# An encoder layer on one core: squares of x moved behind the last rounding of the first gate's input, transposes moved ahead, one product copied by ScalarE

## The chip, the core and the metric

One NeuronCore of one Trainium2 chip. The metric is the device time of one execution of the whole kernel in microseconds, the median of several runs. The engines are named as in the profile: PE is TensorE (matmuls), PEld its weight loads, DVE VectorE, ACT ScalarE, POOL GpSimd, SP SyncE, which only issues DMAs here. Each engine works through its own instructions in order.

## The reference

x is 512 x 2048 in float32, one batch and one layer.

```
h  = rms_norm(x, pre_mix_g);  z = h @ w_in                      # [q | k | v | u]
m  = concat(chunked_attention(q, k, v), multiscale_pool(u)) @ w_o
x  = x + rms_norm(m, post_mix_g)
h  = rms_norm(x, pre_ffn_g)
up = causal_dwconv(h @ w_up)                                    # 2048 x 11264, 3 taps
y  = (gelu(up[:, :5632]) * up[:, 5632:]) @ w_down               # 5632 x 2048
x  = x + rms_norm(y, post_ffn_g)
```

## The kernel before, in words

**Products.** Every float32 operand is split into a rounded high part and the rest (`split`, lines 133 to 141: ScalarE rounds on line 135, or on 138 with a gain per channel; VectorE subtracts on line 136, or 139). A product of a pair is three matmuls, high x high, low x high and high x low (`mm3`, lines 151, 153, 154; the first needs only the high parts, and the second of the gate's matmuls needs the low part of the activations). The larger products are Winograd's form of Strassen's scheme: seven products P1 to P7 of half-size blocks, whose sums VectorE, ScalarE and accumulating DMAs make.

**The order of the work.** TensorE's order is the order of the code. The order on the other engines is planned when the program is built, from modelled times: an instruction of later code can go ahead of one of earlier code that isn't ready. `tc.issue_after(ins)` gives each instruction traced in its block an edge of order to `ins`, if it is on the engine of `ins`; no semaphore is waited on for that. Buffers are tiles in rings: a new tile waits until the readers of the one whose place it takes are done. PSUM has eight banks, each a tile of 128 x 512.

**The first gate (lines 705 to 786).** After the output projection's last product, the rows of x are finished in two halves of 256 tokens. For each half `norm` makes the scale, `x2` (line 715) adds the normed projection to x, `turn_back` (lines 723 to 733) transposes x block by block on TensorE and rounds it into the tiles `gT` with the gain (lines 138, 139), and `keep_x` (lines 717 to 721) squares x on ScalarE for the next norm, two halves of a row block at a time through one scratch tile `junk` (lines 643 to 645), and stores x by SP. The squares' sums are added on line 787; the factor from them is used only behind the second `up` product's start, when `spread2` transposes it (line 213, tile `R`).

The first unit's gate, h @ w_up, is made in two halves of tokens so that it can begin before the second half of x is there (`gate_part(q, t0)`, lines 762 to 767): four weight blocks q of four channel blocks each, two output blocks j, so 24 matmuls of 256 columns for a q and half. The code makes all four parts of the first half; then in five steps it adds x (`x2`, columns of step q), transposes four channel blocks of the second half (8 transposes), and from the second step on multiplies the part of the step before. The first 16 transposes so stand side by side on TensorE. `keep_x(2)` stands behind these steps in the code. Behind the gate come the first unit's other product (`ups[1]`, line 785) and the sums of `gT` for Winograd's scheme (line 1028).

**The first chunk of the down projection (lines 876 to 926 and 1296 to 1312).** The contraction over 5632 is cut into five chunks of 1024 and a rest. In a chunk there are seven products for each of two column halves cc, 24 matmuls of 512 columns each (`multiply`). In chunk 0 their order is `ORDER0`: P1 of both halves, P2 of both, P5, P6, P3, P7, P4. Products accumulate in chains of two banks: P1, P6, P7 and P4 in `pa`, P5 and P3 in `pg`, P2 in `pd`. With P1's two chains kept open, P2's four banks are the ones that P5 takes next: P5 of the second half waits until `pd` of the second half is read. `keep_product` reads the banks: P1, P5 and P6 are copied by ScalarE (`copied`, line 900); for P2 and P3 VectorE adds the banks to the copy kept before (line 909). The copies are tiles of a ring of five, `part`. The result is added to a DRAM sum by a DMA that GpSimd issues (lines 923, 925). Factors are made `AHEAD` = 3 products in advance, so that the roundings for the products to come (`bh`, `bl`, `ah`, `al`) stand in the code ahead of a product's `keep_product`.

**The end.** `last` makes the last rest's blocks of 128 rows; the final row block has columns cut 512, 512, 512, 256, 256. When its norm is known, line 1403 adds each piece to x on VectorE and line 1404 stores it by SP. The pieces are taken in order of their width, the narrowest first.

Of the kernel before, what the change touches and what calls it, by code (L numbers as in the profile page):

```python
# [17 lines left out]
D = 2048  # L18
# [21 lines left out]
V_PREFFN = V_PREMIX + KD  # L40
# [5 lines left out]
def f32(ap):  # L46
    return ap.bitcast(F32)
# [28 lines left out]
def encoder_layer(ctx: ExitStack, tc: tile.TileContext, x, xT, vecs, rel, post_mix, post_ffn,  # L76
# [7 lines left out]
    nc = tc.nc  # L84
# [16 lines left out]
    def bank(name):  # L101
        return psum.tile([P, 512], F32, tag="ps", name=name)
# [27 lines left out]
    def col(v, i):  # L130
        return vec[:, v + i:v + i + 1]

    def split(hi, lo, src, scale=None):
        if scale is None:
            rounded = nc.scalar.activation(hi, src, AF.Copy)  # L135
            rest = nc.vector.tensor_sub(lo, src, f32(hi))  # L136
        else:
            rounded = nc.scalar.activation(hi, src, AF.Copy, scale=scale)
            rest = nc.vector.scalar_tensor_tensor(lo, src, scale, f32(hi), op0=ALU.mult, op1=ALU.subtract)
        split.last, split.rest = rounded.ins, rest.ins  # L140
        return rounded.ins
# [35 lines left out]
    def new_hT(name):  # L177

        return [new_pair(f"{name}{i}", 4, S) for i in range(4)]
# [7 lines left out]
    def new_gT():  # L187
        return [big.tile([P, 4, 4, S // 2], F32R, tag="hT", bufs=4, name=f"gT{i}") for i in range(4)]

    def g_half(gT, kb, t):  # L190
        return tuple(gT[kb // 4][:, kb % 4, at, :] for at in AT[t])
# [5 lines left out]
    def part(w, *idx):  # L197
        return tuple(v[(slice(None),) + idx] for v in w)
# [24 lines left out]
    def qk_specs(h):  # L223
        return halves(f"q{h}", w_in, head_cols("q", h), 8, P), halves(f"k{h}", w_in, head_cols("k", h), 8, P)
# [45 lines left out]
    for h in range(1, HEADS):  # L270
        q, k = qk_specs(h)
# [57 lines left out]
    hT = new_hT("hT")  # L329
# [5 lines left out]
    for kb in range(KD):  # L335
        i, o = divmod(kb, 8)
# [22 lines left out]
    with tc.tile_pool(name="p1", bufs=2, reuse_waits="tile") as p1:  # L359
# [216 lines left out]
        T = S // 2  # L576
# [41 lines left out]
    with tc.tile_pool(name="p2", bufs=1, reuse_waits="tile") as p2:  # L618
# [9 lines left out]
        ssq2, rm = (small[:, i:i + 8].rearrange("p (a b) -> p a b", a=NT) for i in (16, 24))  # L628
# [3 lines left out]
        def columns(cc):  # L632
            return slice(cc * 512, (cc + 1) * 512)
# [9 lines left out]
        def square(v, total):  # L643
            junk = p2.tile([P, D // 2], F32, tag="junk", name="junk")
            nc.scalar.activation(junk[:, :v.shape[-1]], v, AF.Square, accum_out=total)
# [59 lines left out]
        xn = {}  # L705
# [8 lines left out]
                v = xn[t0 + t][:, l * D // 2 + cs.start:l * D // 2 + cs.stop]  # L714
                nc.vector.scalar_tensor_tensor(v, y[:, t, cs], rm[:, t0 + t, l:l + 1], v, op0=ALU.mult, op1=ALU.add)

        def keep_x(t0):
            for t in range(t0, t0 + 2):
                for l in range(2):
                    square(xn[t][:, l * D // 2:(l + 1) * D // 2], ssq2[:, t, l:l + 1])  # L720
                nc.sync.dma_start(x2d[t - 2] if t >= 2 else out[t * P:(t + 1) * P, :], xn[t])

        def turn_back(t0, pair):

            ps = bank(f"xt{t0}_{pair}")
            for k in range(2):
                kb = 2 * pair + k
                for t in range(2):
                    nc.tensor.transpose(ps[:, k * T + t * P:k * T + (t + 1) * P],
                                        xn[t0 + t][:, kb * P:(kb + 1) * P], ident)  # L730
            for k in range(2):
                kb = 2 * pair + k
                split(*g_half(hT, kb, t0 // 2), ps[:, k * T:(k + 1) * T], col(V_PREFFN, kb))

        whole = slice(0, D // 2)
        for cc in range(2):
# [4 lines left out]
        hT = new_gT()  # L741
# [17 lines left out]
        ups = [[bank(f"up0_{p}_{j}") for j in range(2)] for p in range(2)]  # L759
        gate_w = []  # L760

        def gate_part(q, t0):
            sl = slice(t0 * P, t0 * P + T)
            for kb in range(4 * q, 4 * q + 4):
                for j in range(2):
                    mm3(ups[0][j][:, sl], part(gate_w[q], j, slice(kb % 4 * P, (kb % 4 + 1) * P)), g_half(hT, kb, t0 // 2),
                        kb == 0, kb == KD - 1)

        for q in range(4):
            gate_w.append(weights.get(f"w00_{q}", 3 - q))  # L770
            gate_part(q, 0)
        for q in range(5):
            if q < 4:
                x2(2, (y21, y22)[q // 2], q // 2, columns(q % 2))
                for i in range(2):
                    turn_back(2, 2 * q + i)
            if q:
                gate_part(q - 1, 2)
                weights.prefetch(q)
        keep_x(2)  # L780
        for q in range(4):
            w = weights.get(f"w10_{q}")
            for kb in range(4 * q, 4 * q + 4):
# [109 lines left out]
    def keep_product(c, cc, i):  # L893

        ps = chains[cc, CHAIN[i]]

        def copied():
            v = later["part"]("part")
            for t in range(2):
                nc.scalar.activation(v[:, t, :], ps[t], AF.Copy)  # L900
            return v

        if i in (1, 5, 6):
            kept[cc, i] = copied()
            return
        if i in (2, 3):
            v = kept.pop((cc, {2: 1, 3: 6}[i]))
            for t in range(2):
                nc.vector.tensor_add(v[:, t, :], ps[t], v[:, t, :])  # L909
        else:  # L910
            v = copied()
            if i == 7:
                five = kept.pop((cc, 5))
                nc.vector.tensor_add(flat(v), flat(five), flat(v))
        if i in (2, 3, 4):
            del chains[cc, CHAIN[i]]
        n = ENDS[i]
        if (c, cc) == (NC - 1, 1) and i in (2, 4):
            not_stored[n] = v
            return  # L920
        dest = sums[n][:, cc * S:(cc + 1) * S].rearrange("(t p) n -> p t n", p=P)
        if (n, cc) in begun:
            nc.gpsimd.dma_start(dest, v, accum_op=ALU.add)  # L923
        else:
            nc.gpsimd.dma_start(dest, v)
            begun.add((n, cc))

    def flat(v):
        return v.rearrange("p a b -> p (a b)")

    with tc.tile_pool(name="p3", bufs=2, reuse_waits="tile") as p3:
# [74 lines left out]
        T = S // 2  # L1006
# [218 lines left out]
    with tc.tile_pool(name="p4", bufs=2, reuse_waits="tile") as p4:  # L1225
# [138 lines left out]
        parts, scaled, ssqs, befores = [[] for _ in range(NT)], [[] for _ in range(NT)], {}, {}  # L1364

        def last(t, cols):
            ps = bank(f"yl{t}")[:, :cols.stop - cols.start]
            for i in range(2):
                last_block(ps, i, t, cols)
            if not parts[t]:  # L1370
                ssqs[t] = piece("ssq", 3, 5)
            ssq, n = ssqs[t], len(parts[t])
            v = y[t][:, cols]
            width = cols.stop - cols.start
            (nc.vector.tensor_add if cols.stop <= C else nc.vector.tensor_sub)(v, ps, v)
            junk = product_part("junk").rearrange("p a b -> p (a b)")
            nc.scalar.activation(junk[:, :width], v, AF.Square, accum_out=ssq[:, n:n + 1])
            if cols.start % C == 0 and t < 2:
                scaled[t].append(row((slot_h, slot_l)[t], f"vg{t}"))
            elif cols.start == 0:  # L1380
                v2 = right_tile(("wl", "wh")[t - 2], f"vg{t}", F32).rearrange("p a b -> p (a b)")
                scaled[t] += [v2[:, :C], v2[:, C:]]
            vg = scaled[t][cols.start // C][:, cols.start % C:cols.start % C + width]
            last.mul = nc.vector.tensor_mul(vg, v, gains[cols.start // C][:, cols.start % C:cols.start % C + width]).ins
            parts[t].append((cols, vg))
            if cols.stop < D and blocks(t)[n + 1].stop == D:
                befores[t] = piece("s3", 3, 1)
                nc.vector.reduce_sum(befores[t], ssq[:, :n + 1], axis=AX.X)
                nc.vector.tensor_scalar(befores[t], befores[t], 1.0 / D, EPS, op0=ALU.mult, op1=ALU.add)
            if cols.stop < D:  # L1390
                return
            r = piece("s1", 3, 1)
            nc.vector.scalar_tensor_tensor(r, ssq[:, n:n + 1], 1.0 / D, befores[t], op0=ALU.mult, op1=ALU.add)
            nc.gpsimd.tensor_tensor(r, r, mhalf[:, :1], op=ALU.pow)
            if t < 2:
                for i in range(2):
                    v = scaled[t][i]
                    nc.scalar.activation(v, v, AF.Copy, scale=r)
                    nc.gpsimd.dma_start(out[t * P:(t + 1) * P, i * C:(i + 1) * C], v, accum_op=ALU.add)
                return  # L1400
            for cols, vg in sorted(parts[t], key=lambda p: p[0].stop - p[0].start):
                res = x2_last[t - 2][cols.start // 1024][:, cols.start % 1024:(cols.stop - 1) % 1024 + 1]
                nc.vector.scalar_tensor_tensor(res, vg, r, res, op0=ALU.mult, op1=ALU.add)
                nc.sync.dma_start(out[t * P:(t + 1) * P, cols], res)

        for n in ("11", "12", "21", "22"):
            for t in range(2):
                at = y[t + 2 * int(n[0]) - 2]
                l = int(n[1]) - 1
                load_sum(n, t, at[:, l * C:(l + 1) * C])  # L1410
                if n in not_stored:
                    v = at[:, l * C + S:(l + 1) * C]
# [56 lines left out]
```

## Time and profile before

| | us |
|---|---|
| three timed runs, median (lowest to highest) | 1881.79 (1881.34 to 1882.3) |
| the profiled execution | 1885.39 |
| its span, first to last instruction | 1883.6 |
| TensorE busy in the span | 1868.9 |
| VectorE busy | 1417.9 |
| ScalarE busy | 1001.6 |
| GpSimd busy | 287.0 |

The mean granted clock of TensorE is 0.997 of full speed. In lines of the profile, "out<-in" are tiles by their names in the program, x16 means that 16 instructions are merged in the row, and a bracket at the end is the idle time of the engine just before and what ended it. A timeline row has the start and the length in us; matmuls overlap, so the length of one is more than the step from one to the next.

### The profile page before, as it was taken

What the parts mean: (1) busy time and instruction counts of PE and PEld (TensorE: products, weight loads), DVE (VectorE), ACT (ScalarE), POOL (GpSimd) and SP (SyncE); (2) the same over time, 40 slices, a digit from 0 to 9 for tenths busy, and PEclk for the clock granted to TensorE, in tenths of its full rate; (3) what the DMA queues carried; (4) which work ended last, traced back from release to release, by engine and by line L of the source; (5) the groups of instructions that cost most, each with busy time, mean ns of one, the idle gap of its engine ahead of it and who ended that gap; (6) DMA issues with size and microseconds to landing.
All of it is one profiled execution on the core that took longest, in us unless ns stands there. A gap on an engine that the chain in (4) does not pass through costs nothing.

```text
span 1883.6 us, 24695 instructions
## 1 busy us (share of the span) xinstructions
PE 1868.9 (99%) x9438; PEld 1595.4 (85%) x9438; DVE 1417.9 (75%) x1608; ACT 1001.6 (53%) x1261; POOL 287.0 (15%) x388
## 2 busy tenths in 40 slices
PE   9999999999999999999999999999999999999998
PEld 7888888888888888888888888888888788888886
DVE  5554445587598657888888888888887799889886
ACT  6333333346465345656656666665665665565553
POOL 4301011000000102121121212222121011111111
PEclk9999999999999999999999999999999999999999
DMA  8799599359796948889888888988889877876885
GB/s 295 244 251 239 159 266 239 105 151 330 225 301 221 241 145 188 204 203 204 199 203 200 207 208 199 199 199 209 209 172 298 325 230 178 206 201 169 181 232 156
DMA packets 181990, 404.47 MB, mean 215 GB/s; under 512 B 11312, under 2 KB 62384, under 8 KB 176560
## 3 DMA queue, kind: packets, MB, share of 16 engines
q0 software_dynamic: 50384, 150.49, 41.5%
q1 hardware_dynamic: 131488, 252.41, 40.0%
q8 instruction: 74, 1.21, 0.3%
q14 instruction: 44, 0.36, 0.1%
HBM read 356.72 MB, written 96.47 MB: 241 GB/s over the span
## 4 chain that ended last, share of the span: by engine, by line
PE 96%; DVE 1%; ACT 1%; DMA 1%; issue 0%; SPq 0%; POOL 0%; POOLq 0%; DVEq 0%; ACTq 0%
PE qa L159 14%; PE qa L165 8%; PE qg L159 7%; PE pa L153 4%; PE pa L154 4%; PE pa L151 4%; PE qg L165 4%; PE qd L159 4%; PE m L154 3%; PE m L153 3%; PE m L151 3%; PE up L153 2%; PE up L154 2%; PE up L151 2%; PE pg L151 2%; PE pg L153 2%
## 5 line engine op out<-in xcount | busy, mean ns | idle before, releaser
L159 PE MATMUL qa<-gT,wfh 128*128 128x512 f32 x912 | 228.3, 392 | 0.0
L136 DVE TENSOR_TENSOR wfl<-wx,wfh 128x1024 fp32r<-128x1024 f32 x152 | 185.9, 1223 | 52.8 <-ACT wfh L135 37.2
L135 ACT ACTIVATE wfh<-wx 128x1024 fp32r<-128x1024 f32 x152 | 161.0, 1059 | 118.6 <-PE qg L159 46.4
L159 PEld LDWEIGHTS qa<-gT,wfh 128*128 128x128 f32 x912 | 164.1, 189 | 29.4
L1092 POOL DMA_DIRECT2D wx<-in_w_up x113 | 96.9, 857 | 451.3 <-DVE wfl L136 430.1
L159 PE MATMUL qg<-h,wfh 128*128 128x512 f32 x608 | 150.4, 389 | 0.1
L136 DVE TENSOR_TENSOR bl<-b,bh 128x2048 fp32r<-128x2048 f32 x56 | 126.9, 2287 | 17.3 <-ACT bh L135 11.7
L135 ACT ACTIVATE bh<-b 128x2048 fp32r<-128x2048 f32 x56 | 106.1, 1914 | 62.4 <-DVE b L859 26.4
L159 PEld LDWEIGHTS qg<-h,wfh 128*128 128x128 f32 x608 | 113.9, 188 | 23.9 <-ACT zb L1149 0.5
L135 ACT ACTIVATE wfh<-wy 128x1024 fp32r<-128x1024 f32 x76 | 80.6, 1061 | 93.1 <-PE qg L159 53.0
L165 PE MATMUL qa<-gT,wfl 128*128 128x256 f32 x912 | 127.7, 283 | 0.0
L151 PE MATMUL pa<-bh,ah 128*128 128x512 f32 x320 | 124.5, 389 | 0.0
L153 PE MATMUL pa<-bl,ah 128*128 128x512 f32 x320 | 124.5, 389 | 0.0
L154 PE MATMUL pa<-bh,al 128*128 128x512 f32 x320 | 124.5, 389 | 0.0
L165 PEld LDWEIGHTS qa<-gT,wfl 128*128 128x128 f32 x912 | 119.9, 191 | 3.3 <-ACT zm L1153 0.2
L136 DVE TENSOR_TENSOR wfl<-wy,wfh 128x1024 fp32r<-128x1024 f32 x76 | 92.8, 1221 | 5.6 <-PE qa L159 1.5
L136 DVE TENSOR_TENSOR wfl<-wz,wfh 128x1024 fp32r<-128x1024 f32 x38 | 46.6, 1227 | 55.3 <-PE qa L159 52.2
L165 PEld LDWEIGHTS qg<-h,wfl 128*128 128x128 f32 x608 | 82.9, 190 | 5.9
L165 PE MATMUL qg<-h,wfl 128*128 128x256 f32 x608 | 84.8, 282 | 0.0
L923 POOL DMA_DIRECT2D sum<-part x30 | 36.2, 1206 | 262.4 <-DVE part L909 194.7
L159 PE MATMUL qa<-h,wfh 128*128 128x512 f32 x304 | 76.1, 392 | 0.0
L159 PE MATMUL qd<-gT,wfh 128*128 128x512 f32 x304 | 75.1, 389 | 0.0
(541 smaller groups left out, 4702.4 us busy)
## 6 DMA issues: line engine op xcount, KB each, us to landing
wx<-in_w_up POOLq DMA_DIRECT2D x113, 512.0 KB, 6.0
b<-in_w_down SPq DMA_DIRECT2D x32, 1024.0 KB, 7.0
wx<-in_w_up SPq DMA_DIRECT2D x40, 512.0 KB, 5.5
wz<-in_w_up SPq DMA_DIRECT2D x38, 512.0 KB, 5.9
wy<-in_w_up SPq DMA_DIRECT2D x38, 512.0 KB, 4.6
wy<-in_w_up POOLq DMA_DIRECT2D x38, 512.0 KB, 5.8
sum<-part POOLq DMA_DIRECT2D x38, 512.0 KB, 8.0
wt<-in_w_o POOLq DMA_DIRECT2D x16, 1024.0 KB, 11.6
```

The source lines that it names most:

```text
L135: rounded = nc.scalar.activation(hi, src, AF.Copy)
L136: rest = nc.vector.tensor_sub(lo, src, f32(hi))
L151: nc.tensor.matmul(ps, l[0], r[0], start=first, stop=False, skip_group_check=onto)
L153: nc.tensor.matmul(low, l[0], r[1], start=False, stop=False, skip_group_check=onto)
L154: nc.tensor.matmul(ps, l[1], r[0], start=False, stop=last, skip_group_check=onto)
L159: nc.tensor.matmul(ps, w[0][:, kb], pairs[kb][0], start=fresh and not kb, stop=last, skip_group_check=not fresh)
L165: nc.tensor.matmul(ps[:, sl], w[1][:, kb], pair[:, sl], start=False, stop=last, skip_group_check=not fresh)
L923: nc.gpsimd.dma_start(dest, v, accum_op=ALU.add)
L1092: nc.gpsimd.dma_start(self.raw[k, what], self.block(k, m, kh), accum_op=ALU.add)
```

## The change

```
-        def keep_x(t0):
+        def keep_x(t0, behind=None):
             for t in range(t0, t0 + 2):
                 for l in range(2):
-                    square(xn[t][:, l * D // 2:(l + 1) * D // 2], ssq2[:, t, l:l + 1])
+                    with tc.issue_after(behind) if behind else nullcontext():
+                        square(xn[t][:, l * D // 2:(l + 1) * D // 2], ssq2[:, t, l:l + 1])
...
-                split(*g_half(hT, kb, t0 // 2), ps[:, k * T:(k + 1) * T], col(V_PREFFN, kb))
+                turn_back.last = split(*g_half(hT, kb, t0 // 2), ps[:, k * T:(k + 1) * T], col(V_PREFFN, kb))
...
-        def gate_part(q, t0):
+        def gate_part(q, t0, some=slice(0, 4)):
-            for kb in range(4 * q, 4 * q + 4):
+            for kb in range(4 * q + some.start, 4 * q + some.stop):
...
         for q in range(4):
             gate_w.append(weights.get(f"w00_{q}", 3 - q))
-            gate_part(q, 0)
+            if q < 3:
+                gate_part(q, 0)
+        gate_part(3, 0, slice(0, 2))
         for q in range(5):
             if q < 4:
                 x2(2, (y21, y22)[q // 2], q // 2, columns(q % 2))
                 for i in range(2):
                     turn_back(2, 2 * q + i)
+            if not q:
+                gate_part(3, 0, slice(2, 4))
             if q:
                 gate_part(q - 1, 2)
                 weights.prefetch(q)
-        keep_x(2)
+        keep_x(2, turn_back.last)
...
         if i in (2, 3):
             v = kept.pop((cc, {2: 1, 3: 6}[i]))
-            for t in range(2):
-                nc.vector.tensor_add(v[:, t, :], ps[t], v[:, t, :])
+            if (c, cc, i) == (0, 1, 2):
+                other = copied()
+                nc.vector.tensor_add(flat(v), flat(other), flat(v))
+            else:
+                for t in range(2):
+                    nc.vector.tensor_add(v[:, t, :], ps[t], v[:, t, :])
...
-            for cols, vg in sorted(parts[t], key=lambda p: p[0].stop - p[0].start):
+            for cols, vg in sorted(parts[t], key=lambda p: p[0].start - p[0].stop):
```

The four squares of the second half of x get an edge behind the last ScalarE rounding of `turn_back`. The last part of the first half's product is cut in two, 12 matmuls each, with the first 8 transposes of the second half between them; the next 8 follow the second 12. P2 of the second column half in chunk 0 is copied out of its banks by ScalarE into a tile of the ring `part` of its own, and VectorE adds that tile to the kept copy. The last row block's pieces are added and stored widest first.

## The prediction

> **What bounds the kernel now.** I read the page first, then TensorE's waits, then the busy time by stretches around each wait, and last the instructions in order of time there.
>
> ```profile
> span 1883.6 us, 24695 instructions
> PE 1868.9 (99%) x9438; PEld 1595.4 (85%) x9438; DVE 1417.9 (75%) x1608; ACT 1001.6 (53%) x1261; POOL 287.0 (15%) x388
> PE pg L151 <- DVE part L909: 2.0, 1, 2.0
> PE up L151 <- ACT gT L138: 1.7, 1, 1.7
> 576.00:580.00 4.00, 2.32 (x20) 1.96 (x18) 3.02 (x6) 2.49 (x6) 0.00 (x0) 1.00 0.38 156
> 580.00:584.00 4.00, 3.71 (x19) 3.23 (x18) 2.58 (x9) 4.00 (x11) 0.36 (x1) 0.74 0.94 395
> 1472.00:1476.00 4.00, 2.10 (x10) 1.41 (x8) 4.00 (x5) 3.83 (x4) 0.00 (x0) 1.00 1.04 397
> 1476.00:1480.00 4.00, 3.90 (x10) 3.15 (x11) 4.00 (x4) 2.00 (x2) 0.72 (x1) 0.57 1.06 429
> ```
>
> TensorE is busy 99% of the span, so only its own waits and its clock are worth anything. Two waits stand out, 1.7 us before the first gate product and 2.0 us in the first chunk of the down projection. In the stretches (length, then PE, PEld, DVE, ACT, POOL, granted clock, DMA share, GB/s) each is followed by a fall of the granted clock, to 0.74 and to 0.57 of four microseconds. Of all 4 us stretches of the span these are the only places, and what adjoins them, with a clock under 0.99 ahead of the last microseconds. The change touches both places, and the order of the last stores.
>
> **Part 1, the first gate.** In order of time:
>
> ```profile
> 573.22 0.28 PE L151 MATMUL up<-gT,w_3h 128*128 128x256 f32 x1
> 573.31 5.38 DVE L715 SCALAR_TENSOR_TENSOR x<-y,small,x 128x512 f32<-128x512 f32 x8
> 576.10 1.91 PE L729 MATMUL xt<-ident,x 128*128 128x128 f32 x16
> 578.13 1.06 ACT L645 ACTIVATE junk<-x 128x1024 f32<-128x1024 f32 x1 [1.51 <-DVE x L715]
> 579.18 0.46 ACT L138 ACTIVATE gT<-xt,vec 128x256 fp32r<-128x256 f32 x1
> 579.67 0.48 DVE L139 SCALAR_TENSOR_TENSOR gT<-xt,vec,gT 128x256 fp32r<-128x256 f32 x1 [0.98 <-ACT gT L138]
> 579.69 0.38 PE L151 MATMUL up<-gT,w_0h 128*128 128x256 f32 x1 [1.68 <-ACT gT L138]
> 580.21 0.39 PE L153 MATMUL up<-gT,w_0h 128*128 128x256 f32 x1
> 582.17 0.41 PE L153 MATMUL up<-gT,w_0h 128*128 128x256 f32 x1
> 582.38 0.41 PE L154 MATMUL up<-gT,w_0l 128*128 128x256 f32 x1
> 585.34 1.04 PE L729 MATMUL xt<-ident,x 128*128 128x128 f32 x8
> 586.14 0.37 PE L151 MATMUL up<-gT,w_1h 128*128 128x256 f32 x1
> 589.90 0.36 PE L151 MATMUL up<-gT,w_2h 128*128 128x256 f32 x1
> ```
>
> The transposes are done by about 577.9, but ScalarE stands in a square of x (578.13) that itself waited 1.51 us for VectorE's eight residual sums, and rounds the first transposed block only at 579.18. TensorE resumes at 579.69, waits again for the low part (580.21), and from about 582 runs at a step of 0.21 us where the product before it made 24 matmuls in 576.10 - 573.22 = 2.88 us, 0.12 each. The whole loss: 16 transposes and 24 matmuls took 585.34 - 576.10 = 9.24 us here; the same work one step later (8 transposes, 24 matmuls, 8 transposes, from 585.34 to 589.90) took 4.56. So **4.7 us** are lost, of which about 1.7 to the half clock.
>
> The change takes the four squares out of the way and sends the first 8 transposes ahead of the last 12 matmuls of the half product. TensorE reaches them at 573.22 + 12 x 0.12 = 574.66. They need the first two residual sums: eight in 5.38 us, one of 0.745, is a step of 0.66, so the second ends at about 574.72. I charge 0.2 us of waiting. Transposes to 575.7 (8 in 586.14 - 585.34 = 0.80), 12 matmuls to 577.1, 8 transposes to 577.9; one more change between the two kinds costs 0.1 (589.90 - 585.34 less 2 x 0.80 and 2.88 is 0.08). ScalarE, with nothing ahead, rounds block 0 by 576, so the high part is in time.
>
> The low part is VectorE's, and the residual sums hold VectorE to 578.69. If all eight stay ahead, the low part of block 0 ends at 578.69 + 0.48 = 579.17 and TensorE idles about 1.25 us; if it is put among them as soon as it is ready (about 576), nothing. The gain is 4.7 - 0.3 - 1.25 = 3.1 or 4.7 - 0.3 = 4.4. VectorE's order is the planner's, and no row of before shows which it is: at 576 four of the eight sums are still to come, so the low part can fall between them, perhaps a sum or two late. I take **3.7**, the middle.
>
> The moved squares: four of 1.06 us, each with a read of its sum, now start behind the last rounding near 593 and end by about 602 even if every weight rounding goes first. Who waits:
>
> ```profile
> 596.09 1.06 ACT L135 ACTIVATE w_3h<-w_3r 128x1024 fp32r<-128x1024 f32 x1 [2.09 <-PE up L153]
> 606.92 0.39 PE L151 MATMUL up<-gT,w_2h 128*128 128x512 f32 x1
> 623.40 0.44 PE R L213 x4
> ```
>
> Behind them in ScalarE's queue stands the rounding of 596.09 and one like it just before, whose blocks are first used at 606.92 or later, 10 us of cover and more; VectorE's sum of the squares and GpSimd's root are needed at 623.40, more than 20 us later. Both uses come some 4 us earlier after the change; the cost is still nothing. The two stores of x on SP's queue read x alone and don't wait for the squares. If the cover were gone, it would cost at most the 4.3 us of the squares.
>
> **Part 2, the second P2.** In the first chunk:
>
> ```profile
> 1468.50 0.39 PE L151 MATMUL pg<-bh,ah 128*128 128x512 f32 x1
> 1473.72 0.39 PE L154 MATMUL pg<-bh,al 128*128 128x512 f32 x1
> 1476.10 0.65 PE L151 MATMUL pg<-bh,ah 128*128 128x512 f32 x1 [2.00 <-DVE part L909]
> 1483.26 0.39 PE L151 MATMUL pa<-bh,ah 128*128 128x512 f32 x1
> 1474.13 1.22 DVE L136 TENSOR_TENSOR al<-s,ah 128x1024 fp32r<-128x1024 f32 x1
> 1475.27 1.28 DVE L909 TENSOR_TENSOR part<-pd,part 128x512 f32<-128x512 f32 x2
> 1472.05 1.06 ACT L135 ACTIVATE ah<-s 128x1024 fp32r<-128x1024 f32 x1 [0.98 <-DVE s L1263]
> 1473.02 1.90 ACT L135 ACTIVATE bh<-t 128x2048 fp32r<-128x2048 f32 x1
> 1474.82 1.06 ACT L900 ACTIVATE part<-pg 128x512 f32<-128x512 f32 x2
> ```
>
> The product that ended at 1468.50 leaves its two banks to the one due at 1473.95 (24 matmuls, a step of 5.22/23 = 0.227). VectorE empties them only at 1475.27, behind operations for later products, the last of them that of 1474.13. The product then runs from 1476.10 to 1483.26, 7.16 us instead of 5.45, since the clock is half for a part. Loss: 1483.26 - 1473.95 - 5.45 = **3.86 us**.
>
> With the change ScalarE copies (2 x 0.53 us as in the row of 1474.82) and VectorE adds from SBUF later, 1.22 us in place of 1.28. The copies are ready at 1468.5. In the order of the code they stand behind the rounding of 1472.05 and ahead of that of 1473.02; the last place that gives ends the first copy at 1473.6, before the bank is wanted. Ahead of that, all is hidden. ScalarE has 1.06 us more to do; what it delays, the rounding of 1473.02, is for a product that starts after 1484. I take **3.8**, with 0 if they fall behind 1473.02.
>
> **Part 3, the last stores**, not in the title but in the diff:
>
> ```profile
> 1877.23 2.87 DVE L1403 SCALAR_TENSOR_TENSOR x<-vg,s,x 128x256 f32<-128x256 f32 x5 [0.72 <-POOL s L1394]
> 1880.12 0.33 SPq L1404 DMA_DIRECT2D out<-x  x1
> out<-x SPq DMA_DIRECT2D x7, 256.0 KB, 2.4
> out<-x SPq DMA_DIRECT2D x2, 128.0 KB, 2.0
> ```
>
> The same five sums end at the same time; the last store has 128 KB, 2.0 us to landing instead of 2.4. Three large stores before it could still be under way, so I take 0.3 (0 to 0.4).
>
> **The sum** is 3.7 + 3.8 + 0.3 = 7.8 us. The profiled execution took 1885.39 us (span 1883.6), the three timed runs have a median of 1881.79; a wait of TensorE weighs the same in both, so 1885.39 becomes 1877.6 and the median 1881.79 - 7.8 = **1874.0**. The terms' ends are 3.1 to 4.4, 3.6 to 3.9 and 0 to 0.4, so 1873.1 to 1875.1.
>
> **Rivals.**
> (1) *VectorE takes ScalarE's place and the clock still falls*: all eight sums stay ahead, 1.25 us of idling, and 1.7 us of half clock remain. Total gain 1.4 + 3.8 + 0.3 = 5.5: 1876.3. Against it: 1.25 us is under the 1.7 and 2.0 us that went ahead of the two falls. [...]
> (2) *The half clock is not the idling's doing* and comes at both places anyway. 1.7 us at each stay: gain 7.8 - 3.4 = 4.4, 1877.4. [...] Against it: the only two long waits are the only two falls.
> (3) *Part 2 does nothing*, because the planner sets the copies behind the rounding of 1473.02: the bank is free at about 1475.4, as before. Gain 4.0: 1877.8.
> (4) *Slower*: the copy takes one of the five tiles of the ring "part".
>
> ```profile
> 1493.65 1.28 ACT L900 ACTIVATE part<-pa 128x512 f32<-128x512 f32 x2 [2.35 <-PE pa L154]
> 1494.83 1.91 ACT L135 ACTIVATE bh<-t 128x2048 fp32r<-128x2048 f32 x1
> DMA to landing us min/median/max: 3.1/7.8/8.4
> ```
>
> The copy of 1493.65 then needs the tile of this P2, which is free when VectorE has added and its store has landed, some 8 us more. Behind it on ScalarE stands the rounding of 1494.83, for the product due at about 1506.6. With 1.1 + 1.9 + 2.3 us of copy and roundings the store must land by 1501 and the sum be made by 1493, else TensorE waits by as much. Nothing holds VectorE's sum any more, so the planner may leave it late; past about 1501 all 7.8 us are lost, and at 1505 the time is 1886. Against it: VectorE made it at 1475 before.
> (5) *The change does not do what it says*: the new edges or the moved transposes leave the order as it was, 1881.5. The edge is between two operations of ScalarE, so this is hardly likely.
>
> **Chances.** Forecast 0.66, (1) 0.09, (2) 0.05, (3) 0.08, (4) 0.08, (5) 0.04. A measurement can tell about 0.2% from no change, 3.8 us: faster means under 1878.0. (3) lies on that bound, half to each side: faster 0.66 + 0.09 + 0.05 + 0.04 = 0.84, same 0.04 + 0.04 = 0.08, slower 0.08. The range goes from 1872.6, all terms at their best with half a microsecond for the spread of runs, to 1878.2, which takes in (1), (2) and most of (3), and leaves out (4) and (5).
>
> **What would show it.** In the changed profile: no wait "up <- gT" over 0.7 us and no "pg <- part" at all among TensorE's waits; granted clock 1.00 throughout until the tail; squares on ScalarE behind 590, eight transposes near 574.8; two copies out of pd on ScalarE before 1470; 128x256 sums last. The forecast is wrong if a new wait of TensorE over 1 us appears in either place, or if a fall of the clock stands where no wait is.

## The result, and the profile after

| | before | after |
|---|---|---|
| median of 11 timed runs, us | 1882.45 | 1877.71 |
| lowest to highest, us | 1881.34 to 1883.78 | 1876.59 to 1881.26 |
| span of the profiled execution, us | 1883.6 | 1876.5 |

The ratio is 0.9977, 95% interval 0.9967 to 0.9986: by the ratio faster by 4.3 us (2.6 to 6.2); the medians differ by 4.7. Forecast were 1874.0 us and a gain of 7.8; 1877.71 lies in the range, near its upper end. The spans of the two profiled executions differ by 7.1 us, much more than the medians. That gap is what the experiments are about.

From the page of the changed kernel and the list of TensorE's waits (line, what it waited for: us in total, times, longest):

```profile
span 1876.5 us, 24700 instructions
PE 1864.2 (99%) x9438; PEld 1592.8 (85%) x9438; DVE 1418.1 (76%) x1607; ACT 1002.3 (53%) x1263; POOL 287.1 (15%) x388
PE qa L165 <- ACT zm L1162: 0.9, 1, 0.9
PE up L153 <- DVE gT L139: 0.6, 1, 0.6
```

Both long waits of before are gone. At the gate a wait for VectorE's low part has come in place of that for ScalarE; in the first chunk there is none. (The wait of 0.9 us on L165 stands at 819 us, in a stage that the change leaves alone; in a second profile of this kernel it is not there.)

The gate in order of time, changed kernel:

```profile
572.94 5.38 DVE L715 SCALAR_TENSOR_TENSOR x<-y,small,x 128x512 f32<-128x512 f32 x8
573.33 0.28 PE L151 MATMUL up<-gT,w_3h 128*128 128x256 f32 x1
574.77 1.04 PE L730 MATMUL xt<-ident,x 128*128 128x128 f32 x8
575.41 0.92 ACT L138 ACTIVATE gT<-xt,vec 128x256 fp32r<-128x256 f32 x2 [4.97 <-PE xt L730]
577.07 1.04 PE L730 MATMUL xt<-ident,x 128*128 128x128 f32 x8
577.86 0.36 PE L151 MATMUL up<-gT,w_0h 128*128 128x256 f32 x1
578.25 0.87 DVE L139 SCALAR_TENSOR_TENSOR gT<-xt,vec,gT 128x256 fp32r<-128x256 f32 x2
578.78 0.38 PE L153 MATMUL up<-gT,w_0h 128*128 128x256 f32 x1 [0.55 <-DVE gT L139]
589.27 1.05 ACT L645 ACTIVATE junk<-x 128x1024 f32<-128x1024 f32 x1
592.30 0.40 PE L151 MATMUL up<-gT,w_0h 128*128 128x512 f32 x1
```

ScalarE rounds the first block at 575.41, right behind the first transposes, and has to do with squares only from 589.27. All eight residual sums still stand ahead of the first low part on VectorE (578.25), and TensorE waits for it.

The first chunk, changed kernel:

```profile
1465.28 0.39 PE L151 MATMUL pg<-bh,ah 128*128 128x512 f32 x1
1467.27 1.06 ACT L905 ACTIVATE part<-pd 128x512 f32<-128x512 f32 x2
1469.35 1.90 ACT L135 ACTIVATE bh<-t 128x2048 fp32r<-128x2048 f32 x1
1471.60 1.22 DVE L915 TENSOR_TENSOR part<-part 128x1024 f32<-128x1024 f32 x1
1476.16 0.39 PE L151 MATMUL pa<-bh,ah 128*128 128x512 f32 x1
```

The copies end at 1468.33, before the banks are wanted at 1470.7; the two P5 products take 1476.16 - 1465.28 = 10.88 us, twice 5.44, with no gap. In before they took 1483.26 - 1468.50 = 14.76.

**A table by stage.** In each profile I cut the span at three matmuls that all of them have: "gate" runs from the first matmul with `w_3h` of the first half's product to the first 128x512 matmul of `ups[1]` (573.33 and 592.30 above), "chunk" from the first `pg` to the next `pa` (1465.28 and 1476.16). Microseconds; "sums" is the start of VectorE's residual sums (the additions of `x2`) counted from the gate's start, and the last column goes by the span, which is given to a tenth:

| kernel | sums | gate | between | chunk | to the end |
|---|---|---|---|---|---|
| before, as profiled | +0.09 | 22.79 | 872.49 | 14.76 | 400.34 |
| before, second profile | -0.90 | 21.24 | 872.20 | 12.56 | 400.39 |
| last stores alone | -0.89 | 21.24 | 873.01 | 12.50 | 400.32 |
| copy alone | -0.33 | 21.81 | 872.88 | 10.88 | 400.40 |
| gate alone | -0.76 | 18.58 | 872.08 | 12.80 | 400.35 |
| squares alone | -0.48 | 19.02 | 872.54 | 12.57 | 400.38 |
| transposes alone | -0.36 | 21.15 | 872.08 | 12.71 | 400.41 |
| changed kernel | -0.39 | 18.97 | 872.98 | 10.88 | 400.34 |
| changed, second profile | -0.20 | 19.16 | 872.23 | 10.88 | 400.31 |
| sums behind, two profiles | -0.92, -0.36 | 17.84, 17.84 | 871.99, 872.80 | 10.88, 10.88 | 400.33, 400.34 |
| squares twice | -0.92 | 23.33 | 872.09 | 12.65 | 400.34 |
| copy four times | -0.91 | 18.45 | 872.15 | 12.18 | 400.33 |
| copy eight times | -0.08 | 19.28 | 871.98 | 19.14 | 400.25 |

The profiled execution of before that the prediction was made from is the dearest of its kind in both stages. Most of the other profiled executions took somewhat less than the median of their kernel (the second of before 1880.93 us against 1882.1, the second of the changed kernel 1876.94 against 1878.54). That holds for kernels with and without the change, so rows of this table are compared with each other and not with a median.

### The profile page after: what moved, and what is told of

Read it like the earlier page. It is cut to its first block, busy times and chain, and to the rows that moved or that the text cites. A ratio compares the mean times of both kernels' runs of the same rounds, so it can differ in the third digit from the quotient of the medians.

```text
span 1876.5 us, 24700 instructions
## 1 busy us (share of the span) xinstructions
PE 1864.2 (99%) x9438; PEld 1592.8 (85%) x9438; DVE 1418.1 (76%) x1607; ACT 1002.3 (53%) x1263; POOL 287.1 (15%) x388
## 4 chain that ended last, share of the span: by engine, by line
PE 97%; DVE 1%; DMA 1%; ACT 1%; issue 0%; SPq 0%; POOL 0%; DVEq 0%; POOLq 0%; ACTq 0%
PE qa L159 15%; PE qa L165 8%; PE qg L159 7%; PE pa L151 4%; PE pa L154 4%; PE pa L153 4%; PE qg L165 4%; PE qd L159 4%; PE m L151 3%; PE m L153 3%; PE m L154 3%; PE up L153 2%; PE up L154 2%; PE up L151 2%; PE pg L151 2%; PE pg L154 2%
## 5 line engine op out<-in xcount | busy, mean ns | idle before, releaser
L165 PE MATMUL qa<-gT,wfl 128*128 128x256 f32 x912 | 127.7, 283 | 0.9 <-ACT zm L1162 0.9
L165 PEld LDWEIGHTS qa<-gT,wfl 128*128 128x128 f32 x912 | 119.9, 191 | 4.2 <-ACT zm L1162 1.1
L165 PEld LDWEIGHTS qg<-h,wfl 128*128 128x128 f32 x608 | 82.9, 190 | 5.9
L165 PE MATMUL qg<-h,wfl 128*128 128x256 f32 x608 | 84.8, 282 | 0.0
L932 POOL DMA_DIRECT2D sum<-part x30 | 36.2, 1206 | 262.0 <-DVE part L918 192.7
```

What stands on the lines that cost most here:

```text
L165: nc.tensor.matmul(ps[:, sl], w[1][:, kb], pair[:, sl], start=False, stop=last, skip_group_check=not fresh)
```

## The experiments

**The kernel before, a second profile.** No edit.

> The kernel before, unchanged, as a second look at it. Theory A (the profiled 7.1 us of span are real in every execution, and something new takes 2.4 us back in the timed runs): the two waits of TensorE of 1.7 and 2.0 us are there again, each followed by a half clock of 3.4 us, and the span is 1883 to 1884 us. Theory B (the profiled execution of before was a costly one, and others lose less): at least one of the two falls of the clock is missing or shorter, and the span is 1880 to 1881.5 us. Time against before: same, within 0.1%.

Measured: 1882.1 us beside 1882.15 (ratio 0.9998, 0.9989 to 1.0007), span of the profile 1879.2. Its TensorE waits and the stretches with the two places:

```profile
PE pg L151 <- DVE part L909: 1.4, 1, 1.4
PE up L151 <- ACT gT L138: 1.1, 2, 0.7
576.00:580.00 4.00, 3.15 (x22) 2.39 (x20) 2.10 (x4) 3.27 (x8) 0.00 (x0) 1.00 0.64 266
580.00:584.00 4.00, 3.32 (x24) 2.85 (x24) 2.93 (x9) 3.38 (x9) 1.01 (x1) 1.00 0.62 260
1472.00:1476.00 4.00, 2.75 (x12) 2.31 (x13) 4.00 (x5) 2.95 (x4) 0.73 (x1) 1.00 1.07 411
```

The same program waits 1.4 and 1.1 us here instead of 2.0 and 1.7, and the granted clock (third column from the end) stays 1.00 in both places. Neither fall came. Theory B holds, the profile of before was a costly execution, though the span is a little under the range that B gave (1880 to 1881.5).

**Gate alone** (the first four hunks of the diff).

> Part 1 alone. The changed kernel's trace has the same work 3.4 us shorter here, with 0.55 us of waiting for VectorE left. Theory A: 3.0 to 3.6 us faster than before, clock 1.00 at the gate, one fall left in the first chunk. Theory B: 1.7 to 2.5 us faster, since the half clock's 1.7 us are not in every execution of before.

Measured: 1879.31 us, ratio 0.9984 (0.9975 to 0.9993), 3.0 us; gate 18.58, chunk as before at 12.80. The interval, 1.3 to 4.7 us, takes in the ranges of both theories; by the table, 21.24 to 21.81 became 18.58, a gain of 2.7 to 3.2. The fall that Theory A expected in its first chunk did not come.

**Copy alone** (the hunk in `keep_product`).

> Part 2 alone: no wait for the banks of pd, the copies on ScalarE ahead of the next rounding. Theory A: 3.5 to 3.9 us faster than before, one fall of the clock left, at the gate. Theory B: 2.0 to 2.8 us faster.

Measured: 1880.83 us, ratio 0.9993 (0.9984 to 1.0002), 1.3 us, not clear of nothing; less than either theory said. Its chunk has no loss, 10.88 instead of the 12.50 to 12.80 of the kernels without the copy: 1.6 to 1.9 us. Copies and roundings on ScalarE:

```profile
1469.67 1.07 ACT L900 ACTIVATE part<-pd 128x512 f32<-128x512 f32 x2
1470.77 1.06 ACT L135 ACTIVATE ah<-s 128x1024 fp32r<-128x1024 f32 x1
1471.74 1.90 ACT L135 ACTIVATE bh<-t 128x2048 fp32r<-128x2048 f32 x1
```

**The last stores alone** (the hunk in `last`).

> Part 3 alone: the last row block's pieces widest first. Both theories: 0 to 0.4 us faster, which the timed runs can hardly tell from nothing; in the trace the time from the last vector operation to the end of the span is 0.2 to 0.4 us shorter than the 3.5 us of before.

Measured: 1882.12 us, ratio 1.0003 (0.9994 to 1.0012). A miss: 400.32 us to the end where the second profile of before has 400.39, no difference at a tenth. The profile of the changed kernel shows why, in its DMA issues (KB each, median us to landing):

```profile
1870.13 2.87 DVE L1412 SCALAR_TENSOR_TENSOR x<-vg,s,x 128x512 f32<-128x512 f32 x5 [0.72 <-POOL s L1403]
out<-x SPq DMA_DIRECT2D x3, 256.0 KB, 2.4
out<-x SPq DMA_DIRECT2D x2, 128.0 KB, 2.5
```

The small stores, issued last and right behind the large ones, now take 2.5 us instead of 2.0. From the last sum (1873.00 here, 1880.10 before) to the end of the span it is 3.5 us in both.

**The two halves of the gate's part.** Squares alone:

```
-        keep_x(2)
+        keep_x(2, turn_back.last)
```

> The four squares behind the last rounding, the transposes left as before. Looks at before and its unchanged parts show 3.1 to 4.7 us lost at the gate, the changed kernel 0.8 to 1.2. Theory A (ScalarE's squares are the whole delay, VectorE's residual sums are done before the low part is wanted): 2.3 to 3.0 us faster than before, like both halves of part 1 together, loss at the gate under 1.2 us. Theory B (the moved transposes are needed, since the low part waits for all eight sums in any case): 1 to 2 us faster, loss at the gate about 2 us.

Transposes alone:

```
+        gate_part(3, 0, slice(0, 2))
         for q in range(5):
...
+            if not q:
+                gate_part(3, 0, slice(2, 4))
```

> The first 8 transposes amid the first half's product, the squares left where the planner puts them (two stand between the first three roundings). Theory A: 0.5 to 1.5 us faster, since squares still stand ahead of the rounding. Theory B: 2 us faster or more.

Measured: squares alone 1880.07 us, ratio 0.9984 (0.9975 to 0.9993), the same as both halves together; gate 19.02. Transposes alone 1881.52 us, 0.9996 (0.9987 to 1.0005); gate 21.15. ScalarE's order with the squares alone, then with the transposes alone:

```profile
576.20 1.35 ACT L138 ACTIVATE gT<-xt,vec 128x256 fp32r<-128x256 f32 x3 [6.50 <-PE xt L730]
578.02 1.62 ACT L138 ACTIVATE gT<-xt,vec 128x256 fp32r<-128x256 f32 x4 [0.47 <-DVE gT L139]
```

```profile
575.70 0.46 ACT L138 ACTIVATE gT<-xt,vec 128x256 fp32r<-128x256 f32 x1
577.31 1.06 ACT L645 ACTIVATE junk<-x 128x1024 f32<-128x1024 f32 x1 [1.15 <-DVE x L715]
578.36 0.82 ACT L138 ACTIVATE gT<-xt,vec 128x256 fp32r<-128x256 f32 x2
```

With the squares gone, seven roundings come with no square between them. With only the transposes moved, a square that waits 1.15 us for VectorE still stands between the first rounding and the next. Theory A holds for the squares, except that it took VectorE's sums to be done in time: TensorE waits 0.7 us in two pieces for the low part there, which VectorE begins at 577.51, when the sums are done. For the transposes the timed gain, 0.75 us by the ratio, is at the lower end of what Theory A said, and the interval takes in no gain at all.

**Residual sums behind the first low parts**, on top of the changed kernel. The last four sums, those of the third and the fourth step, get an edge behind a low part: `first_rests` holds the two operations of VectorE (`split.rest`) that make the last low part of the first and of the second `turn_back` of the first step. The diff is cut to the line that uses them:

```
-                x2(2, (y21, y22)[q // 2], q // 2, columns(q % 2))
+                x2(2, (y21, y22)[q // 2], q // 2, columns(q % 2), first_rests[q - 2] if q > 1 else None)
```

> The changed kernel with the last four residual sums put behind the first low parts on VectorE (the third step's behind the first pair's, the fourth step's behind the second pair's). If the rest of the wait at the gate is VectorE's eight sums, the wait 'up L153 <- DVE gT' of 0.2 to 0.6 us goes and the loss at the gate falls from 0.8 to 1.2 to about 0.3 us: 0.5 to 0.9 us faster than the changed kernel, 0.9970 to 0.9976 of before. If the later transposes then wait for the delayed sums, the same as the changed kernel or slower.

```profile
572.04 2.73 DVE L716 SCALAR_TENSOR_TENSOR x<-y,small,x 128x512 f32<-128x512 f32 x4
575.54 1.51 DVE L139 SCALAR_TENSOR_TENSOR gT<-xt,vec,gT 128x256 fp32r<-128x256 f32 x3 [0.77 <-ACT gT L138]
576.97 0.74 DVE L716 SCALAR_TENSOR_TENSOR x<-y,small,x 128x512 f32<-128x512 f32 x1
576.00:580.00 4.00, 4.00 (x37) 4.00 (x36) 3.90 (x10) 2.69 (x6) 0.00 (x0) 1.00 0.00 1
```

Four sums, then low parts and sums in turn; TensorE is busy for the whole of 576 to 580, and no wait at the gate is left in its list. The gate takes 17.84 us in both profiles, 1.1 to 1.3 less than in the changed kernel. Its span, 1874.0, is the lowest of all. In the timed runs: 1878.14 us, 0.9972 (0.9961 to 0.9983), and once more on a chip with the changed kernel beside it:

> The changed kernel once more, to stand beside the next one on the same chip: 0.9970 to 0.9985 of before, no fall of the clock ahead of the tail, 0.8 to 1.2 us lost at the gate, nothing in the first chunk.

> The changed kernel with the last four residual sums behind the first low parts, once more. Its profile showed 0.03 us lost at the gate; if that holds in the timed runs it is 0.8 to 1.1 us faster than the changed kernel beside it. If the earlier medians (1878.14 and 1877.71) are the truth, the two can't be told apart, and the spread of the rest of the kernel hides it.

Measured: changed kernel 1878.54 us, 0.9979 (0.9970 to 0.9988); with the sums behind 1876.43, 0.9969 (0.9958 to 0.9980). Both times it has the better ratio, by 0.5 and 1.0 thousandths, 0.9 and 1.9 us, but the intervals overlap: shown in the profile, likely but not settled in the timed runs.

**Squares twice**, on the kernel before:

```
+                    for _ in range(2 if t0 else 1):
                         square(xn[t][:, l * D // 2:(l + 1) * D // 2], ssq2[:, t, l:l + 1])
```

> Each of the four squares is computed twice (the second writes the same value), the order of the rest as the planner sets it: two squares more stand ahead of the first roundings. Theory A (the half clock comes from the idling, and whether it comes depends on how much of a fixed stretch of 3.4 us is idle): the wait at the gate grows by 1 to 2 us, and the clock falls there in this profile as in that of before; 2.5 to 4 us slower than before. Theory B (the falls in the profile of before had another cause): the wait grows, no fall of the clock; 1 to 2 us slower.

Measured: 1885.17 us, ratio 1.0016 (1.0007 to 1.0025), 3.0 us slower. That is the time of Theory A, but its profile has no fall of the clock, as in Theory B, and the first wait hardly grew; the added squares were spread over later roundings instead, and TensorE waited there:

```profile
PE up L153 <- DVE gT L139: 1.5, 2, 0.9
PE up L151 <- ACT gT L138: 1.4, 2, 0.9
592.00:596.00 4.00, 2.50 (x19) 2.07 (x18) 4.00 (x7) 2.01 (x4) 0.00 (x0) 1.00 0.34 93
```

The gate takes 23.33 us, 2.1 more than at the same start of the sums. So squares ahead of roundings cost time, both ways; for the clock this run decides nothing, since the idling at the gate came in short pieces, 0.9 us at the longest.

**A wait of known length.** In the changed kernel the copy of P2 is written several times, so that TensorE gets the banks late:

```
-        def copied():
+        def copied(times=1):
...
-            for t in range(2):
+            for t in [t for _ in range(times) for t in range(2)]:
```

> The changed kernel with ScalarE's copy of the second P2 written four times over, so that the banks come free late and TensorE idles about 1.1 us where the changed kernel idles nothing. Theory A (the half clock comes where less than some four tenths of a fixed stretch of 3.41 us is busy: shares of 0.31 and 0.37 fell in the looks so far, 0.47 and more did not): no fall, whatever the phase; 1.1 us slower than the changed kernel. Theory B (the falls are not the idling's doing): no fall either, the same 1.1 us.

> The same with eight copies: TensorE idles about 5 us in one piece, so that at every phase one stretch of 3.41 us is less than four tenths busy. Theory A: the clock falls here in this and every execution, for one or two stretches of 3.41 us, and the time is the idling plus 1.7 us or more: 6.5 to 9 us slower than the changed kernel. Theory B: no fall; 5 us slower.

Measured: copied four times, 1879.11 us, 0.9982 (0.9973 to 0.9991), chunk 12.18 (1.3 more than without the wait), no fall; 0.6 us over the changed kernel's 1878.54 in the timed runs. Copied eight times, 1885.29 us, 1.0015 (1.0007 to 1.0024), 6.75 us over it:

```profile
PE pg L151 <- ACT part L905: 5.1, 1, 5.1
1472.00:1476.00 4.00, 1.16 (x3) 0.97 (x4) 1.50 (x2) 4.00 (x8) 0.00 (x0) 0.76 1.06 433
1476.00:1480.00 4.00, 4.00 (x11) 3.13 (x10) 2.83 (x2) 4.00 (x5) 0.73 (x1) 0.50 1.01 426
1480.00:1484.00 4.00, 4.00 (x17) 3.20 (x17) 0.72 (x1) 1.92 (x4) 0.00 (x0) 0.88 1.02 426
```

A wait of 5.1 us, and the clock falls: half for 0.48 x 4 + 4 + 0.24 x 4 = 6.9 us. The chunk takes 19.14, 8.26 more than without the wait, of which about 3 are the clock. The timed runs' 6.75 is more than the wait alone and less than this. All eleven of them have a mean granted clock of 0.997, where nine of the changed kernel's eleven beside them have 0.999, which speaks for the fall in each. Idling of 5.1 us in one piece did bring the half clock here: Theory A.

## Why the prediction was right, and where its sizes were not

**The mechanisms** came as told. Part 1: ScalarE's squares were what delayed the rounding; without them VectorE's sums are late next, by the path that the text gave as "all eight stay ahead". Part 2: the copies stand behind one rounding and ahead of the next, and the wait is gone. The squares behind the last rounding cost nothing.

**The sizes against the profile it was made from** came too: there the gate lost 22.79 - 18.97 = 3.82 us (said: 3.7), the chunk 14.76 - 10.88 = 3.88 (said: 3.8), the end 0 (said: 0.3).

**The step that failed** is the one in the sum: "a wait of TensorE weighs the same in both". The profiled execution stood 3.6 us above the median, and I carried its waits over to the median without asking whether that excess lay in them. It did, for a good part. In kernels whose gate is that of before and has no half clock it takes 21.24, 21.24 and 21.81 us, in the five with both halves of part 1 and the sums left alone 18.45 to 19.28 (mean 18.89): 2.5 us in place of 3.7, and 2.8 at the same start of the sums (22.14 plus that start against 19.36 plus it, each to 0.02 us in all eight profiles). The six unchanged chunks without a fall take 12.50 to 12.80 (mean 12.63) and become 10.88: 1.75 in place of 3.8. The sum is 4.3 (4.5 at the same start), what the ratio of the timed runs says (2.6 to 6.2).

What the profiled execution had more: at the gate its sums began 1.0 us later than in the second profile, which the gate pays in full (why this start varies isn't shown), and the half clock cost about 0.6 (22.79 less 22.14 + 0.09) where the prediction put 1.7, since TensorE would have waited for roundings meanwhile anyway. In the chunk the wait was 0.5 us longer (2.0 against 1.4 to 1.6) and the half clock cost the other 1.6.

How often the clock falls in the timed runs can be told roughly from their mean granted clocks, which are on record to a thousandth; by the traces a fall of 3.41 us takes 0.0009 off. Of the 91 timed runs of before beside the experiments, 46 have 0.999 (mean time 1882.0 us), 31 have 0.998, which profiles without a fall ahead of the tail have too, and 14 have 0.997 (mean 1883.1), the value of the profiled execution. So at least half have no fall, and two falls are the exception. None of the 91 took as long as the profiled 1885.39 us; the longest took 1885.34.

**Luck in the number.** The terms' own ends gave 1873.1 to 1875.1, and the measured 1877.71 lies outside them. It lies in the stated range because that was drawn to take in the times of rivals (1) to (3), which were put at 1876.3, 1877.4 and 1877.8 and which did not happen as told. The profiles, and not the time, say that the mechanisms were right.

**The choice of 3.7 as a middle** between "all eight sums ahead" (3.1) and "among them" (4.4): it was the first. At the start of the sums that the profile of before had, the changed gate would take 19.36 + 0.09 = 19.45 us, an estimate from the table, and gain 3.3, near the 3.1 of that case. Putting the sums behind the low parts removes the wait: 17.84.

**The moved transposes** were worth little: squares alone give 19.02 where 19.36 - 0.48 = 18.88 is the length with both. With the squares still in the way they bring 0.6 by the table (22.14 - 0.36 = 21.78 against 21.15).

**The last stores**: the 0.3 assumed that a small store lands as soon as it does alone. It did not behind the large ones (2.5 us in place of 2.0).

**The rivals.** (1) was half right: VectorE took ScalarE's place, but no clock fell. (2) did not come: the changed kernel has no fall in either place, and with eight copies, which made TensorE idle 5.1 us, one came back. (3), (4) and (5) did not come: VectorE's addition to the kept copy is made at 1471.60, and no copy waited for a tile of its ring.

## What to carry to other kernels

Before a sum is made from one profiled execution, compare its own time with the timed median: an excess of the size of the gain that one forecasts may be those very waits, and a second profile of the unchanged kernel tells. On an engine that serves a path late, look at what the planner puts between the operations of the path; an edge of order (`issue_after`) that moves work whose result isn't needed for another 10 us costs a few lines, and the next engine on the path wants the same look.

## What the runs showed of the hardware that was not expected

**The clock fell in stretches of one length.** In before the half clock begins at 581.93, at 1476.22, and at 1879.0 in the idle tail; the first two last 3.41 us each, that with eight copies 6.9, about twice as long. The distances from each start to the next are 894.29 and 402.77 us, 262.0 and 118.0 times 3.413 us. The 3.41 us ahead of the two falls of before were 0.31 and 0.37 busy (matmuls by their steps of 0.12 and 0.23 us), those ahead of the fall with eight copies not at all (the next there count 0.4, and the half clock went on). The length of a wait alone hardly tells them apart: 1.68 us at the gate of before brought a fall, 1.63 us in the first chunk of the kernel with the gate alone did not. The "some four tenths" in Theory A of the wait of known length was an estimate from such shares; no run tried it by itself.

**Transposes in a stretch without a fall.** In the copy-alone kernel the 3.41 us from 576.0 (laid back in steps of 3.413 us from the fall in its tail, an estimate) were 0.50 busy, but 0.04 without the transposes (0.11 us each), and the clock stayed whole: the next matmuls keep steps of 0.12 us, where at the half clock in before they took 0.21. In the second profile of before the shares from 575.4 were 0.63 and 0.12, with the last stores alone from 576.5 they were 0.43 and 0.27, and the clock stayed whole by the same steps. By matmuls alone all three are under the 0.31 that fell; only with the transposes counted are they above the 0.31 and 0.37.
